# A hybrid attention block on one core: two key transposes come a projection chunk later, and two sets of branch weights are fetched tile by tile

## The chip, the core and the metric

The kernel runs on one core of a Trainium2 chip. TensorE (PE) multiplies matrices and transposes, VectorE (DVE), ScalarE (ACT) and GpSimd (POOL) work on rows of elements, and SyncE (SP) issues the transfers between the chip's memory and the core's own. Each engine goes through its own list of instructions in the order in which the program's scheduler put them, and waits there for semaphores of the others. The metric is the time of one execution in microseconds (us); lower is better.

## What is computed

One layer of a decoder block on 1024 tokens of width 1024, in float32. One projection of the normed input gives all that the two attention branches need; the branches are gated, merged and projected, and a SwiGLU feed-forward part follows.

```python
h = rmsnorm(x, norm_mix_g[l])
proj = h @ w_in[l]
(q_a, k_a, v_a, q_i, k_i, w_i, q_b, k_b, v_b, g) = split_columns(proj)
...
k_i = layernorm(k_i, idx_k_norm_g[l], idx_k_norm_b[l])
k_i = apply_partial_rope(k_i[:, :, None, :], cos_i, sin_i)[:, :, 0, :]
o_a = dsa_sparse_attention(q_a, k_a, v_a, q_i, k_i, w_i, n_top)
...
o_b = differential_attention(q_b, k_b, v_b, lam)
...
gates = jax.nn.sigmoid(g + gate_b[l]).reshape(B, S, N_BRANCH, D_MODEL)
merged = (gates[:, :, 0] * (o_a @ w_branch_dsa[l])
          + gates[:, :, 1] * (o_b @ w_branch_diff[l]))
x = x + merged @ w_out[l]
h = rmsnorm(x, norm_ffn_g[l])
gu = h @ w_ffn_in[l]
x = x + (jax.nn.silu(gu[..., :D_FF]) * gu[..., D_FF:]) @ w_ffn_out[l]
```

The sparse branch (DSA, 8 heads of 64) has an indexer: 8 small heads of width 32 score every earlier token (`relu(q_idx . k_idx)` weighted and summed), the 256 highest scores of each row are selected, and attention runs over those. The differential branch has 4 heads with two softmaxes each, whose difference weights the values.

## The kernel before

Every float32 product is made of three products of split operands: `x` is `hi + lo`, and the pairs (hi,hi), (hi,lo) and (lo,hi) of `PASS` are summed. To split a weight tile of 128x1024, ACT copies it to `whi` (L101), and POOL subtracts to get `wlo` (L102). `Weights.get` (L121 to L129) does the transfer (L125) and the split in one call.

**The projection stage.** There are 32 chunks for the queries and keys of both branches, 16 for the values and 16 for the gates. A query or key chunk is `chunk_mm` (L423 to L429): 24 products of 128x512 (L427) into one of the two accumulator banks `mm`, which an ACT copy (L468 for the first two chunks of a branch, L488 for the others) then reads out; DVE makes the low part of the later ones (L489). After each chunk `fill(5.2)` (L443) is called. Its first calls take a function out of the list `extra` (L441); later ones call `pump`, which feeds the indexer's work between the chunks: two pieces of `logits_gen` (the scores of one head) each time, and then as many pieces of `topk_gen` as fill the 5.2 us by its own table of costs. A piece of the top-k is a MAX8 (L299), which finds the eight highest values of each row, and a MATCH_REPLACE8 (L300), which takes them out, both on DVE; there are 176 such pairs. After the gates all that is left of them is run off, then attention starts.

Before the first scores, `idx_kT(0)` and `idx_kT(1)` (L227 to L237) must turn the indexer's keys: an ACT copy (`q`, L229), four PE transposes (L232), an ACT copy into `kst` (L235) and DVE subtractions. The keys come from `idx_keys`, a chain of DVE work (normalisation and rotation, its last instruction L188) that runs beside the first chunk.

**The attention stage.** There are 32 units for the differential branch (4 heads of 8 row blocks) and 64 for the sparse one. A unit's parts run with lags: scores and softmax at lag 0, transposes later, the product with the values at lag 4, and the closing part at lag 7. One loop over all units calls what is due. `diff_D` (L690 to L694) closes the last unit of a head: `finish_T` (L612) transposes the head's rows (L616) into `oT_hi` and `oT_lo` (L622, L623). At head 2 it also fetches the four tiles of `w_bdiff`, the differential branch's output weights. `dsa_D` (L756 to L776) closes the sparse units: at every third of them it makes half a column chunk of the differential branch's output (12 products, L767) out of these tiles, and at the end of `m` = 5 it fetches the four tiles of `w_bdsa`, which the sparse branch's output (`branch`, L625 to L631) needs right behind the last unit. The raw tiles stand in the pool `gst` under the name `gt`, which has two buffers; a head's rows (`rows_tile`, L641) and the gate tiles of the chunks (L761) take the same two.

Of the kernel before, what the change touches and what calls it, by code (L numbers as in the profile page):

```python
# [8 lines left out]
F32 = mybir.dt.float32  # L9
F32R = mybir.dt.float32r  # L10
# [8 lines left out]
P = 128  # L19
# [31 lines left out]
def block_kernel(ctx, tc, x, pos, g_mix, w_qk, w_v, q_scale, w_idx, w_gate, ikg, ikb, lams, sub_g, gate_b,  # L51
# [175 lines left out]
    def idx_kT(g):  # L227
        k4 = ip.tile([P, 4, 4, 32], F32, name="q4", bufs=1)
        A.activation(k4, IX[:, 4 * g:4 * g + 4, None, 256:288].to_broadcast([P, 4, 4, 32]), AF.Copy)  # L229
        tr = tr_bank()  # L230
        for j in range(4):
            T.transpose(tr[:, j, :], k4[:, j].rearrange("p a b -> p (a b)"), ident)  # L232
        ksl = kst[:, g * 512:(g + 1) * 512]
        tf = tr.rearrange("p a b -> p (a b)")
        A.activation(ksl, tf, AF.Copy)  # L235
        for q0 in (32, 96):
            V.tensor_sub(ksl[q0:q0 + 32], tf[q0:q0 + 32], ksl[q0:q0 + 32].bitcast(F32))  # L237
# [200 lines left out]

    fetch(0)
    fetch(1)  # L440
    extra = [lambda: idx_kT(0), lambda: idx_kT(1)]  # L441

    def fill(us):  # L443
        if extra:
# [245 lines left out]
    def diff_D(u):  # L690
        if u.last:
            finish_T(rows_of.pop((0, u.h)), u.h, sg[:, 0:1])
            if u.h == 2:
                u.wb.extend(W2.get(w_bdiff[k], raw=gst.tile([P, S], F32, name="gt")) for k in range(4))  # L694

    def dsa_A(u):
        sv, nh = scores(maps[1, u.m], u.t)
# [58 lines left out]
    def dsa_D(u):  # L756
        if u.chunk is not None:
            c, hf = u.chunk // 2, u.chunk % 2
            if hf == 0:
                u.fill.gt = gst.tile([P, S], F32, name="gt")  # L760
                nc.sync.dma_start(u.fill.gt, gate_dr[8 + c])  # L761
            gt = u.fill.gt[:, hf * 512:hf * 512 + 512]
            bt = mm_bank()
            n = 0
            for k in range(4):
                for a, b in PASS:
                    T.matmul(bt, lhsT=u.wb[k][b][:, c * P:(c + 1) * P],  # L767
                             rhs=oT[a][:, k, hf * 512:(hf + 1) * 512], start=n == 0, stop=n == 11)
                    n += 1
            V.tensor_mul(gt, bt, gt)  # L770
            nc.sync.dma_start(mb_dr[c][:, hf * 512:hf * 512 + 512], gt)
        if u.last and u.m == 2 * PARKED - 1:
            for h in range(PARKED):
                for dr, x_ in zip(o_dr, oT):
                    nc.sync.dma_start(x_[:, h, :].bitcast(F32), dr[h])
            wa.extend(W2.get(w_bdsa[k], raw=gst.tile([P, S], F32, name="gt")) for k in range(4))  # L776

    units, wbd, wa = [], [], []
    for h in range(4):
        for j, t in enumerate(ORDER):  # L780
            u = Unit()
            u.br, u.h, u.t, u.ext, u.first, u.last = 0, h, t, (t + 1) * P, j == 0, j == NT - 1
            u.wb = wbd
            u.f = ((1, diff_X), (0, diff_A0), (3, diff_B), (0, diff_A1), (4, diff_C), (7, diff_D))
            units.append(u)
    fill_ = Unit()
    for m in range(8):
        prs = {}
        for j, t in enumerate(ORDER2):
            u = Unit()  # L790
            u.pr = prs.setdefault(t // 2, Unit())
            u.pr.n = 0
            u.br, u.m, u.h, u.t, u.ext, u.first, u.last = 1, m, m // 2, t, (t + 1) * P, j == 0, j == NT - 1
            u.wb = wbd
            n = 8 * m + j
            u.fill = fill_
            u.chunk = n // EVERY if n % EVERY == 0 and n // EVERY < 2 * KC else None
            u.f = ((0, dsa_A), (1, dsa_X), (2, dsa_B), (4, dsa_C), (7, dsa_D))
            units.append(u)
# [576 lines left out]
```

## Time and profile before

| | |
|---|---|
| median of three runs | 1628.11 us (1628.06 to 1634.58) |
| the profiled execution, its own time | 1631.66 us |
| its span, first to last instruction | 1629.6 us |
| busy: PE, DVE, ACT, POOL | 95%, 71%, 41%, 35% |
| mean granted clock of PE | 0.99 |

The profile's times are those of one execution, counted from its first instruction; 2.06 us of its time lie outside the span. In a row of the timeline the start, the duration, the engine, the line and the operation are followed by what is written and read, and where the engine stood idle before it, by the length of that and what ended it.

### The profile page before, as it was taken

What the parts mean: (1) busy time and instruction counts of PE and PEld (TensorE: products, weight loads), DVE (VectorE), ACT (ScalarE), POOL (GpSimd) and SP (SyncE); (2) the same over time, 40 slices, a digit from 0 to 9 for tenths busy, and PEclk for the clock granted to TensorE, in tenths of its full rate; (3) what the DMA queues carried; (4) which work ended last, traced back from release to release, by engine and by line L of the source; (5) the groups of instructions that cost most, each with busy time, mean ns of one, the idle gap of its engine ahead of it and who ended that gap; (6) DMA issues with size and microseconds to landing.
All of it is one profiled execution on the core that took longest, in us unless ns stands there. A gap on an engine that the chain in (4) does not pass through costs nothing. (4 is left out here: it accounts for less than half of the span.)

```text
span 1629.6 us, 22639 instructions
## 1 busy us (share of the span) xinstructions
PE 1549.3 (95%) x8204; PEld 1319.4 (81%) x8204; DVE 1165.1 (71%) x1880; ACT 670.2 (41%) x1199; POOL 570.4 (35%) x465
## 2 busy tenths in 40 slices
PE   7799999999999998899999989999999999999997
PEld 6688779998888787788788977788787878887886
DVE  6479999989999998788772377555555555745553
ACT  5444541222211887777831243233232322443343
POOL 2442611342210024222421126666566666203311
PEclk9899999999999999999999999999999999999999
DMA  5243243348521466775384132444344445885532
GB/s 173 80 142 119 84 148 123 100 140 230 144 91 52 104 140 146 185 194 158 136 283 169 40 116 107 154 163 165 136 168 153 165 154 194 313 317 181 168 130 104
DMA packets 108079, 247.45 MB, mean 152 GB/s; under 512 B 12480, under 2 KB 30016, under 8 KB 107968
## 3 DMA queue, kind: packets, MB, share of 16 engines
q1 hardware_dynamic: 107968, 246.02, 46.2%
q8 instruction: 64, 1.05, 0.3%
q14 instruction: 47, 0.39, 0.1%
HBM read 167.06 MB, written 78.91 MB: 151 GB/s over the span
## 5 line engine op out<-in xcount | busy, mean ns | idle before, releaser
L102 POOL TENSOR_TENSOR alo<-r,ahi 128x512 fp32r<-128x512 f32 x152 | 206.4, 1366 | 165.3 <-ACT ahi L101 159.7
L102 POOL TENSOR_TENSOR wlo<-raw,whi 128x1024 fp32r<-128x1024 f32 (+1 forms) x49 | 117.5, 2404 | 310.0 <-ACT whi L101 300.6
L101 ACT ACTIVATE ahi<-r 128x512 fp32r<-128x512 f32 x152 | 95.5, 631 | 259.7 <-PE tr L1061 88.1
L1061 PE MATMUL tr<-blk,ahi 128*128 128x512 f32 x528 | 165.4, 394 | 9.2 <-DVE r L1073 8.5
L299 DVE MAX8 m<-score 128x8 f32<-128x640 f32 (+5 forms) x176 | 162.6, 924 | 5.4 <-POOL score L283 0.4
L300 DVE MATCH_REPLACE8 score<-m,score 128x640 f32<-128x640 f32 (+5 forms) x176 | 159.5, 906 | 0.0
L102 DVE TENSOR_TENSOR blk<-r,blk 128x1024 fp32r<-128x1024 f32 x77 | 101.6, 1352 | 73.8 <-ACT blk L101 73.6
L101 ACT ACTIVATE whi<-raw 128x1024 fp32r<-128x1024 f32 (+1 forms) x52 | 53.5, 1032 | 202.7 <-issue 97.7
L1061 PEld LDWEIGHTS tr<-blk,ahi 128*128 128x128 f32 x528 | 98.8, 189 | 33.6 <-DVE r L1073 11.9
L101 ACT ACTIVATE blk<-r 128x1024 fp32r<-128x1024 f32 x77 | 78.1, 1053 | 108.4 <-PE big L1277 44.4
L1061 PE MATMUL big<-blk,ahi 128*128 128x512 f32 x352 | 109.1, 391 | 0.9 <-DVE blk L102 0.9
L427 PE MATMUL mm<-hT_hi,whi 128*128 128x512 f32 x256 | 102.2, 399 | 5.6 <-DVE st_lo L489 5.6
L1061 PE MATMUL mm<-blk,ahi 128*128 128x512 f32 x336 | 104.3, 391 | 0.4 <-ACT r L1070 0.3
L1061 PE MATMUL tr<-blk,alo 128*128 128x512 f32 x264 | 103.6, 393 | 0.6 <-POOL alo L102 0.6
L427 PE MATMUL mm<-hT_lo,whi 128*128 128x512 f32 x256 | 100.6, 393 | 0.0
L427 PE MATMUL mm<-hT_hi,wlo 128*128 128x512 f32 x256 | 100.3, 392 | 0.0
L427 PE MATMUL big<-hT_hi,whi 128*128 128x512 f32 x256 | 99.6, 389 | 0.0
L427 PE MATMUL big<-hT_lo,whi 128*128 128x512 f32 x256 | 99.6, 389 | 0.0
L427 PE MATMUL big<-hT_hi,wlo 128*128 128x512 f32 x256 | 99.6, 389 | 0.0
L1277 PE MATMUL big<-blk 128*128 128x512 f32 x396 | 91.8, 391 | 1.8 <-DVE r L1245 1.5
L1277 PEld LDWEIGHTS big<-blk 128*128 128x128 f32 x396 | 73.8, 188 | 19.5 <-issue 1.9
L592 PE MATMUL big<-khs,qs 128*128 128x512 f32 (+4 forms) x192 | 74.4, 389 | 5.3 <-DVE mx L701 2.5
(286 smaller groups left out, 3973.9 us busy)
## 6 DMA issues: line engine op xcount, KB each, us to landing
r<-in_w_ffi_dram SPq DMA_DIRECT2D x44, 512.0 KB, 4.5
r<-in_w_ffo_dram SPq DMA_DIRECT2D x22, 512.0 KB, 4.8
tdr<-r SPq DMA_DIRECT2D x22, 512.0 KB, 2.6
sdr<-r SPq DMA_DIRECT2D x44, 256.0 KB, 2.6
r<-sdr SPq DMA_DIRECT2D x44, 256.0 KB, 4.0
r<-tdr SPq DMA_DIRECT2D x44, 256.0 KB, 4.0
r<-actdr SPq DMA_DIRECT2D x33, 256.0 KB, 4.1
r<-in_w_ffo_dram SPq DMA_DIRECT2D x33, 256.0 KB, 5.2
```

The source lines that it names most:

```text
L101: A.activation(hi, src, AF.Copy)
L102: lo_eng.tensor_sub(lo, src, hi.bitcast(F32))
L299: tc.keep_in_program_order(V.max(m8, work[t]))
L300: V.match_replace(work[t], m8, work[t], GONE)
L427: T.matmul(dst, lhsT=w[b][:, k * P:(k + 1) * P], rhs=hT[a][:, k, u * 512:(u + 1) * 512], start=n == 0, stop=n == 23)
L592: T.matmul(sp_[:, u, :n], lhsT=q[:, t * P:(t + 1) * P], rhs=kh_[:, cols], start=True, stop=False)
L1061: T.matmul(banks[z], lhsT=w[b][:, k * P:(k + 1) * P], rhs=o[:, a, k, :], start=first and m == 0, stop=last and m == 11, skip_group_check=True)
L1277: T.matmul(bs_[r], lhsT=v[:, a, r * P:(r + 1) * P], rhs=v[:, b, 512:], start=p in OPEN and j == 0 and m == 0, stop=p in SHUT and j == NP - ...
```

## The change

The list of the first fills gets an empty entry in front: the first fill does nothing, the key transposes come with the second and third, and all of the pumping starts one chunk later. And the two fetches of four weight tiles are taken apart by a new function `step`: `n` counts the units from the head's last one on, an even `n` from 0 to 7 issues one tile's transfer, and the odd one behind it does that tile's split, so that four tiles spread over eight units. The number of instructions and bytes is the same.

```diff
-    extra = [lambda: idx_kT(0), lambda: idx_kT(1)]
+    extra = [lambda: None, lambda: idx_kT(0), lambda: idx_kT(1)]
...
     def diff_D(u):
         if u.last:
             finish_T(rows_of.pop((0, u.h)), u.h, sg[:, 0:1])
-            if u.h == 2:
-                u.wb.extend(W2.get(w_bdiff[k], raw=gst.tile([P, S], F32, name="gt")) for k in range(4))
+        step(u.wb, w_bdiff, 8 * u.h + u.j - 23)
+
+
+    def step(wb, src, n):
+        if 0 <= n < 8 and n % 2 == 0:
+            wraw[0] = gst.tile([P, S], F32, name="gt")
+            nc.sync.dma_start(wraw[0], src[n // 2])
+        elif 0 <= n < 8:
+            hi = W2.pool.tile([P, 1024], F32R, name="whi", bufs=W2.n)
+            lo = W2.pool.tile([P, 1024], F32R, name="wlo", bufs=W2.n)
+            tc.keep_in_program_order(A.activation(hi, wraw[0], AF.Copy))
+            G.tensor_sub(lo, wraw[0], hi.bitcast(F32))
+            wb.append((hi, lo))
+
+    wraw = [None]
...
-            wa.extend(W2.get(w_bdsa[k], raw=gst.tile([P, S], F32, name="gt")) for k in range(4))
+        step(wa, w_bdsa, 8 * u.m + u.j - 8 * PARKED * 2 + 1)
```

The scheduler orders each engine's list anew, so the place of the rows is read from the built programs.

ScalarE behind the projection's first two weight tiles: `L229` are the copies ahead of the key transposes, `L409` is a small constant with its table load, `L468` reads a chunk's bank out.

```order
-L229 ACTIVATE q_723<-ix 128x512
+L229 ACTIVATE q_750<-ix 128x512
 L409 ACT_TABLE_LOAD
 L409 ACTIVATE lsm<-lsm 128x2
+L468 ACTIVATE xx<-mm,qs 128x512 x2
+L235 ACTIVATE kst<-tr 128x512
+L229 ACTIVATE q_801<-ix 128x512
+L101 ACTIVATE st_hi<-ra 128x512
+L101 ACTIVATE st_hi<-xx 128x512
+L101 ACTIVATE whi<-raw 128x1024
 L468 ACTIVATE xx<-mm,qs 128x512
 L235 ACTIVATE kst<-tr 128x512
```

The copy for the keys stands at the same place; behind it both of the first chunks are now read out before `kst`, where it was one. On TensorE it is likewise: the second chunk's 24 products stand ahead of the first transposes L232, not behind them.

The transfers that SyncE issues around the four tiles of `w_bdiff` (`qs`, `khs`, `kls` and `vt` are the next heads' queries, keys and values, `odr` parked results). Before:

```order
-L125 DMA gt<-in_w_bdiff_dram 128x1024
-L538 DMA khs<-qkh_77 64x1024
-L539 DMA kls<-qkl_79 64x1024
-L537 DMA qs<-qkl_79 64x1024
-L125 DMA gt<-in_w_bdiff_dram 128x1024
-L538 DMA khs<-qkh_77 64x1024
-L539 DMA kls<-qkl_79 64x1024
-L537 DMA qs<-qkh_77 64x1024
-L125 DMA gt<-in_w_bdiff_dram 128x1024
-L538 DMA khs<-qkh_77 64x1024
-L539 DMA kls<-qkl_79 64x1024
-L546 DMA vt<-vsdr 128x8x128
```

and now, where the second, third and fourth tile are issued:

```order
+L538 DMA khs<-qkh_77 64x1024
+L539 DMA kls<-qkl_79 64x1024
+L546 DMA vt<-vsdr 128x8x128
+L699 DMA gt<-in_w_bdiff_dram 128x1024 x2
+L767 DMA odr_82<-so_6273 64x256
+L767 DMA odr_83<-so_6274 64x256
+L767 DMA odr_82<-so_6358 64x256
+L767 DMA odr_83<-so_6359 64x256
+L537 DMA qs<-qkh_77 64x1024
+L699 DMA gt<-in_w_bdiff_dram 128x1024
```

The second to fourth tile came between the loads of the sparse branch's first head and held them up; now these loads and `vt` go first, and the second and third tile are issued together behind them, the fourth after four small stores.

TensorE at the first chunk of the differential branch's output (`L767`, in the changed kernel `L780`; `L616` is `finish_T` of the last head; `L726` and now `L739` are transposes of the sparse units, `L739` and now `L752` their products with the values). Before, from `finish_T` to the last product of the chunk:

```order
L616 MATMUL tr<-ident,gt 128x128 x8
L767 MATMUL mm<-oT_hi,wlo 128x512
L593 MATMUL big<-kls,qs 128x448
L592 MATMUL big<-khs,qs 128x384
L593 MATMUL big<-kls,qs 128x384
L726 MATMUL tr<-ident,pm 128x128 x5
L767 MATMUL mm<-oT_hi,whi 128x512
L767 MATMUL mm<-oT_lo,whi 128x512
L739 MATMUL mm<-wide,vt 128x256
L592 MATMUL big<-khs,qs 128x512
L593 MATMUL big<-kls,qs 128x512
L767 MATMUL mm<-oT_hi,wlo 128x512
```

and now, where the products of its second tile and the ones behind it stand:

```order
L592 MATMUL big<-khs,qs 128x384
L739 MATMUL tr<-ident,pm 128x128 x2
L780 MATMUL mm<-oT_hi,whi 128x512
L780 MATMUL mm<-oT_lo,whi 128x512
L739 MATMUL tr<-ident,pm 128x128 x4
L780 MATMUL mm<-oT_hi,wlo 128x512
L739 MATMUL tr<-ident,pm 128x128 x2
L780 MATMUL mm<-oT_hi,whi 128x512
L780 MATMUL mm<-oT_lo,whi 128x512
L780 MATMUL mm<-oT_hi,whi 128x512
L780 MATMUL mm<-oT_lo,whi 128x512
L780 MATMUL mm<-oT_hi,wlo 128x512
```

Before, eight of the chunk's twelve products stood ahead of `finish_T` and four behind it, the second chunk's twelve some way on in one piece. Now two stand ahead of `finish_T` and ten behind it, mixed with those of the second chunk, and both chunks end at the same place. From `branch` on TensorE's list is the same as before.

## Rows read from the trace of the kernel before

**Rows 1.** The page's busy times: us, share of the span, instructions.

```profile
PE 1549.3 (95%) x8204; PEld 1319.4 (81%) x8204; DVE 1165.1 (71%) x1880; ACT 670.2 (41%) x1199; POOL 570.4 (35%) x465
```

**Rows 2.** Windows: busy us (instructions) of PE, PEld, DVE, ACT, POOL; then clock, DMA.

```profile
66.00:68.00 2.00, 2.00 (x6) 1.57 (x5) 1.27 (x2) 1.20 (x3) 1.65 (x2) 0.50 0.00 0
120.00:520.00 400.00, 394.36 (x2119) 342.36 (x2119) 383.85 (x563) 113.59 (x151) 109.62 (x66) 1.00 0.39 125
...
650.00:662.00 12.00, 7.52 (x31) 4.88 (x30) 7.41 (x17) 9.22 (x19) 7.40 (x9) 0.87 0.65 170
662.00:665.00 3.00, 3.00 (x15) 2.84 (x14) 1.95 (x7) 1.81 (x6) 0.00 (x0) 0.50 0.30 121
780.00:815.00 35.00, 31.61 (x193) 26.02 (x192) 26.33 (x69) 29.56 (x70) 18.08 (x24) 0.95 0.37 134
815.00:1620.00 805.00, 783.67 (x3820) 656.00 (x3819) 449.24 (x518) 265.59 (x395) 334.86 (x239) 1.00 0.48 169
```

**Rows 3.** Timeline of PE from the first chunk's end to the third chunk's start.

```profile
55.65 0.39 PE L427 MATMUL mm<-hT_lo,whi 128*128 128x512 f32 x1
55.88 0.39 PE L427 MATMUL mm<-hT_hi,wlo 128*128 128x512 f32 x1
64.15 1.12 PE L232 MATMUL tr<-ident,q 128*128 128x128 f32 x4 [7.89 <-ACT q L229]
...
65.49 0.63 PE L427 MATMUL mm<-hT_lo,whi 128*128 128x512 f32 x1
65.92 0.63 PE L427 MATMUL mm<-hT_hi,wlo 128*128 128x512 f32 x1
...
72.51 0.47 PE L427 MATMUL mm<-hT_hi,whi 128*128 128x512 f32 x1
```

**Rows 4.** Timeline of DVE, ACT and POOL beside it.

```profile
62.98 0.45 DVE L188 TENSOR_TENSOR ix<-rope_a,rope_b 128x288 f32<-128x288 f32 x1
...
63.47 0.63 ACT L229 ACTIVATE q<-ix 128x512 f32<-128x512 f32 x1 [6.69 <-DVE ix L188]
...
65.52 0.67 ACT L468 ACTIVATE xx<-mm,qs 128x512 f32<-128x512 f32 x1
...
47.31 4.76 POOL L102 TENSOR_TENSOR wlo<-raw,whi 128x1024 fp32r<-128x1024 f32 x2 [9.49 <-ACT whi L101]
```

**Rows 5.** Timeline of DVE: one wait late in the projections, and the top-k's end.

```profile
362.21 0.94 DVE L300 MATCH_REPLACE8 score<-m,score 128x768 f32<-128x768 f32 x1
367.48 0.84 DVE L528 CAST causw<-caus 128x128 bf16<-128x128 f32 x1 [4.32 <-DMA vsdr<-st_lo]
...
531.03 0.69 DVE L305 TENSOR_SCALAR bias<-score 128x1024 bf16<-128x1024 f32 x1
532.62 1.23 DVE L650 CUSTOM_DVE_ANT_0 pm<-big,causw 128x1024 f32<-128x1024 f32 x1 [0.90 <-PE big L593]
```

**Rows 6.** Timeline of PE where the gates end and attention starts.

```profile
531.18 0.40 PE L427 MATMUL big<-hT_hi,wlo 128*128 128x512 f32 x1
```

**Rows 7.** Timeline of SP, ACT and POOL: the last two tiles of `w_bdiff`.

```profile
653.66 0.33 SPq L125 DMA_DIRECT2D gt<-in_w_bdiff_dram  x1
...
650.12 1.06 ACT L101 ACTIVATE whi<-gt 128x1024 fp32r<-128x1024 f32 x1 [3.23 <-DMA gt<-in_w_bdiff_dram]
...
658.00 1.06 ACT L101 ACTIVATE whi<-gt 128x1024 fp32r<-128x1024 f32 x1 [1.31 <-DMA gt<-in_w_bdiff_dram]
...
659.13 2.38 POOL L102 TENSOR_TENSOR wlo<-gt,whi 128x1024 fp32r<-128x1024 f32 x1 [2.04 <-ACT whi L101]
```

**Rows 8.** Timeline of PE: the first two chunks of the differential branch's output.

```profile
661.57 0.79 PE L767 MATMUL mm<-oT_hi,wlo 128*128 128x512 f32 x1 [0.17 <-POOL wlo L102]
...
669.74 0.39 PE L767 MATMUL mm<-oT_hi,wlo 128*128 128x512 f32 x1
```

**Rows 9.** Timeline of SP and ACT: the last three tiles of `w_bdsa`.

```profile
784.20 12.89 SPq L125 DMA_DIRECT2D gt<-in_w_bdsa_dram  x3
...
800.28 1.06 ACT L101 ACTIVATE whi<-gt 128x1024 fp32r<-128x1024 f32 x1 [1.37 <-DMA gt<-in_w_bdsa_dram]
```

More of the change, by code (lines that the diff above doesn't have):

```diff
@@ L782, in block_kernel @@
             u.br, u.h, u.t, u.ext, u.first, u.last = 0, h, t, (t + 1) * P, j == 0, j == NT - 1
+            u.j = j
             u.wb = wbd
@@ L793, in block_kernel @@
             u.br, u.m, u.h, u.t, u.ext, u.first, u.last = 1, m, m // 2, t, (t + 1) * P, j == 0, j == NT - 1
+            u.j = j
             u.wb = wbd
```

## The prediction

> **What bounds the kernel now.** The page's busy times come first: TensorE is busy for 1549.3 of 1629.6 us [rows 1], so what can be won is some 80 us of its idle time and the time in which it ran at half clock. The windows then tell where. Behind 815 us TensorE is busy for 783.67 of 805 us [rows 2], and its list there is unchanged: that stretch can be shifted, not shortened. From 120 to 520 us, where the projections, the indexer's scores and the top-k lie, TensorE is busy for 394.36 of 400 us and DVE for 383.85 [rows 2]: two engines are full at once, and neither alone sets the time. The two tie at the end too: the last product of the gates ends at 531.58 (531.18 and 0.40, [rows 6]), the last step of the top-k at 531.72 (531.03 and 0.69), and the first softmax of attention starts at 532.62 after 0.90 us in which DVE waits for scores [rows 5]. The three places of the change are at 50 to 75, 627 to 670 and 770 to 815 us.
>
> **The transposes.** The timeline of TensorE shows a stall at 56.27: the first chunk's last product ends there (55.88 and 0.39), and the transposes L232 start at 64.15 after 7.89 us of waiting for the ACT copy `q` [rows 3]. The copy itself waited 6.69 us for the last step of the keys on DVE, which ends at 63.43 [rows 4]. Nothing in the change makes that step earlier. But the second chunk no longer stands behind the transposes: its weights were split by 52.07 (47.31 and 4.76, [rows 4]) and its bank is the free one of two. Its 24 products, 0.23 us apart (55.65 to 55.88, [rows 3]), take 5.5 us, so they run from 56.3 to 61.8, and the stall is 2.35 us instead of 7.89. The transposes then start at 64.15 as before. The third chunk uses the first tile again, but needs the first chunk's bank, which ACT has read out at 66.19 (65.52 and 0.67, [rows 4]): it starts at 66.2, where it was 72.51 [rows 3]. TensorE gains **6.3 us** there.
>
> The clock is the first thing that could take from it. After the stall the granted clock was 0.50, the lower of the two levels (1.2 GHz), between 66 and 68 us [rows 2], and products took 0.63 instead of 0.39 us, 0.43 apart [rows 3]; some ten of them were slow, which is 10 x 0.20 = 2.0 us. The new stall is a third as long, with a second of about one microsecond behind it. I leave the 2.0 us where they are: with no fall at all it would be 2 more, the gain 8.3.
>
> How much of this reaches attention is decided by DVE, since the top-k must be done first. The change takes nothing off DVE; what it can win is its waits, and work that comes earlier. The top-k starts when the first scores are there. These come one chunk later in the list (5.5 us) on a TensorE that is 6.3 us earlier: some 1 us of gain at the start. Next, DVE stands 4.32 us at L528, waiting for the transfers that end the value chunks [rows 5]; these move with TensorE. In the changed program's DVE list 109 MAX8 stand ahead of L528, where it was 111, so DVE arrives two pairs earlier (some 2 us each, the MATCH_REPLACE8 half took 0.94, [rows 5]) and has them still to do behind it. The wait becomes 0.7 to 1 us shorter at best. So the top-k ends about 2 us earlier, and TensorE's gates 6 us earlier. The scores are then ready before DVE is, so its wait of 0.90 us goes as well. Attention starts 2.9 us earlier, and TensorE stands idle there for some 3 us: there are few score banks that it can fill ahead. **Term 1: −2.9 us**; the bounds are 0, if DVE was as full as it can be, and −6.3, if DVE turns out to wait for TensorE in more places than I count.
>
> **The tiles of `w_bdiff`.** In the kernel before, the four tiles go one after the other through one buffer, each waiting for POOL's split of the one before. The last is issued at 653.66, its ACT copy starts at 658.00 after 1.31 us of waiting, and POOL splits it from 659.13 to 661.51 [rows 7]: one round of issue, landing, copy and split is 7.9 us. TensorE waits for this split: the last product of the first chunk starts at 661.57 [rows 8], and the second chunk is done at 670.13 [rows 8]. From 650 to 662 TensorE is busy for only 7.52 of 12 us, and the clock falls: it is 0.50 from 662 to 665, in which 15 instructions fill 3.00 us [rows 2]. So this place costs some 4.5 us of idle time and 1.5 of slow work. ACT, too, is held: it stood 3.23 us at the third tile's copy [rows 7], with `finish_T`'s copies and the softmax's exponentials behind it in its list.
>
> In the new order SyncE first issues the loads of the sparse head and `vt`, then tiles two and three together, and ACT's copies of tiles two to four come behind `finish_T`'s. So `finish_T` no longer waits behind a copy that waits for a transfer: I put it at 650 instead of 653. The third tile lands some 4.3 us behind that (653.66 to 658.00, [rows 7]), at 654.4; POOL ends the second tile's split at 658 and the third's at 660.3. The fourth tile needs the second's buffer, is issued at 658, and by the same round its split ends at 666 (658 and 7.9). The first chunk's last product is thus 4.4 us later than before, but the second chunk's twelve are no longer a block behind it: they are done tile by tile beside the first's, and one or two products are left when the last split comes. Both chunks are done at about 667 instead of 670.1. **Term 2: −3.0 us**, bounds −4.5 (all the idle time) and +2 (a split that comes 5 us later than I put it).
>
> **The tiles of `w_bdsa`.** The last three are issued together from 784.20 on, held for 12.89 us until `gst` buffers come free; the last copy waits 1.37 us, at 800.28 [rows 9]. `branch` starts right behind. From 780 to 815 TensorE is idle for 3.4 of 35 us, and the clock's mean is 0.95 [rows 2]. In the new order three are still issued together, but in ACT's list of the changed program the copies stand 16 to 19 places later and let exponentials go first. **Term 3: −1.0 us**, bounds 0 and −3.
>
> Against this stand no added instructions. The sum is −6.9 us: 1624.8 for the profiled execution of 1631.66. That one lies 3.55 above the median, and I carry the difference over to it: 1628.11 − 6.9 = 1621.2, which I give as 1621.
>
> **The rivals.**
>
> *The top-k hides all of the first gain.* DVE is busy for 96% of the 400 us; if the waits that remain are not TensorE's, term 1 is 0 and the time 1624. Against it speaks the 0.90 us that DVE did wait for scores.
>
> *The whole gain of TensorE survives.* If DVE is late because its inputs were, the 6.3 us carry to attention: 6.3 + 3 + 1 gives 1617.8. For it speaks that DVE waits at L528 for transfers that move with TensorE; against it that the top-k's 176 pairs are not fewer.
>
> *The split tiles come too late, slower.* The third tile's transfer waits for `finish_T`, the fourth's for the second's split, and both splits stand in line on POOL. If each ACT copy is held by another 3.23 us, as one was before [rows 7], the last split ends at 666 + 6.5 = 672.5. TensorE has the products of tiles two to four in list order, so it stands behind the first that is late, and both accumulator banks are held. Then the second chunk ends at 673.5, 3.4 later than before, and if the products left run 0.20 us slow, as above, it is 5 to 6 with some ten to twelve of them. With terms 1 and 3 this is 1628.11 + 5.5 − 3.9 = 1629.7. It turns into a loss for this place when the last split ends behind 669.6, and for the kernel when that is behind 673.
>
> *The clock falls at the new waits.* Idle time moves to the start of attention (3 us) and in between the chunks' tiles. If each of these lets the clock fall for as long as the stall at 56 us did, 2.0 us at one place and 1 to 2 at the other go back: 1621 + 3.5 = 1624.5. The trace bears it out so far in that both stalls of before were followed by a granted clock of 0.50 [rows 2]. The Trainium skill, "TensorE: Matmul & The Clock Gate", section "HAM oscillation — how this bites in real kernels", says that bursts of products with waits for data in between start cold each time, and would so speak against a chunk cut into four pieces; the trace agrees with it at both places, and has no row for pieces as short as these.
>
> **How the numbers follow.** The forecast has a chance of 0.38 (1618.5 to 1623.5 around 1621), the top-k's cover 0.13 (1624), TensorE's whole gain 0.24 (1617.8, and below with the bounds of terms 2 and 3), the late tiles 0.15 (1629.7), the clock 0.10 (1624.5). 0.5% is 8.1 us, about what a measurement of this kernel tells from no change: faster is below 1620.0. That holds for most of TensorE's whole gain and for four tenths of the forecast: 0.24 x 0.95 + 0.38 x 0.4, with a little from elsewhere 0.39. Slower by as much, above 1636.2, would take late tiles at twice the price: 0.03. The rest is 0.58. The range runs from 1614 (6.3, 4.5 and 3 together, 1614.3) to 1629, which leaves out half of the late tiles and a little at the lower end.
>
> **What would show it.** In the profile after: the stall ahead of L232 near 2.4 us and the third chunk at 66; the first softmax some 3 us earlier, TensorE waiting for DVE there; the last split of `w_bdiff` near 663 and both chunks done by 664, once the 2.9 us are taken off; `branch` 6 to 7 us earlier. The prediction is wrong if attention starts at the old place or 6 earlier, or if TensorE waits at L780 for a split for over 3 us.

## The result and the profile after

The changed kernel takes 1618.96 us in the median of 4 runs (1614.87 to 1619.83), beside 1629.18 us before in the same comparison: a ratio of 0.9926 with a 95% interval of 0.9897 to 0.9954, or 10.2 us by the medians and 12.1 by the ratio (its interval is 7.5 to 16.8). The profiled execution has a span of 1617.9 us, 11.7 below that of before.

Read in the order of the prediction. TensorE is busy for the same time in a shorter span (page of the changed kernel; compare [rows 1]):

```profile
PE 1548.1 (96%) x8204; PEld 1318.3 (81%) x8204; DVE 1156.8 (71%) x1880; ACT 669.1 (41%) x1199; POOL 568.7 (35%) x465
```

Its timeline from the second chunk's end to the third chunk's start (compare [rows 3]):

```profile
61.84 0.39 PE L427 MATMUL mm<-hT_hi,wlo 128*128 128x512 f32 x1
64.87 1.11 PE L232 MATMUL tr<-ident,q 128*128 128x128 f32 x4 [2.65 <-ACT q L229]
66.96 0.79 PE L427 MATMUL mm<-hT_hi,whi 128*128 128x512 f32 x1 [0.98 <-ACT xx L468]
67.56 0.63 PE L427 MATMUL mm<-hT_lo,whi 128*128 128x512 f32 x1
```

The stall ahead of L232 is 2.65 us where it was 7.89, with 0.98 more ahead of the third chunk. That chunk starts at 66.96. In this execution the keys were done 0.72 us later than before (their last step ends at 64.15, before at 63.43), so against the keys it came 6.3 us earlier: 72.51 − 63.43 = 9.08 before, 66.96 − 64.15 = 2.81 now. Of these, 0.35 us are a change of order: before, the second four transposes stood ahead of the third chunk, and now they stand behind it (they start at 74.44). Products of 0.63 us follow at a granted clock of 0.50 (68 to 70 us), so the clock fell as before.

DVE's timeline where the projections end, at two of the bias copies L305, and at the top-k's end (compare [rows 5]), and TensorE's last product of the gates (compare [rows 6]):

```profile
360.69 0.83 DVE L528 CAST causw<-caus 128x128 bf16<-128x128 f32 x1 [4.42 <-DMA vsdr<-st_lo]
...
366.97 0.56 DVE L305 TENSOR_SCALAR bias<-score 128x768 bf16<-128x768 f32 x1
...
441.62 0.63 DVE L305 TENSOR_SCALAR bias<-score 128x896 bf16<-128x896 f32 x1
...
524.88 0.69 DVE L305 TENSOR_SCALAR bias<-score 128x1024 bf16<-128x1024 f32 x1
525.91 1.23 DVE L650 CUSTOM_DVE_ANT_0 pm<-big,causw 128x1024 f32<-128x1024 f32 x1 [0.34 <-PE big L593]
...
524.47 0.40 PE L427 MATMUL big<-hT_hi,wlo 128*128 128x512 f32 x1
```

The wait at L528 is as long as before (4.42, 4.32 before) but ends 6.8 us earlier. The first softmax starts at 525.91, 6.7 us earlier, and DVE waits only 0.34 us ahead of it; the gates end at 524.87, before the top-k (525.57). The two L305 in the middle take 0.56 and 0.63 us. What they took before was not among the rows ahead of the prediction; here they are, with POOL beside them, in the timeline of the kernel before:

```profile
369.67 2.47 DVE L305 TENSOR_SCALAR bias<-score 128x768 bf16<-128x768 f32 x1
...
446.22 2.19 DVE L305 TENSOR_SCALAR bias<-score 128x896 bf16<-128x896 f32 x1
...
369.32 2.40 POOL L102 TENSOR_TENSOR wlo<-raw,whi 128x1024 fp32r<-128x1024 f32 x1 [1.08 <-ACT whi L101]
...
445.52 2.40 POOL L102 TENSOR_TENSOR wlo<-raw,whi 128x1024 fp32r<-128x1024 f32 x1 [8.46 <-ACT whi L101]
```

Each begins while POOL is at a split of a weight tile, takes 2.47 and 2.19 us, and ends 0.4 to 0.5 us behind the split.

The windows of the changed kernel, TensorE's columns first, then the clock behind POOL's columns (compare [rows 2]; the later ones are moved by the 6.7 us):

```profile
120.00:520.00 400.00, 397.67 (x2130) 345.70 (x2129) 383.27 (x566) 113.98 (x153) 107.65 (x66) 1.00 0.40 125
...
643.00:655.00 12.00, 9.39 (x54) 7.01 (x54) 10.33 (x24) 10.60 (x23) 7.48 (x11) 1.00 0.39 118
655.00:664.00 9.00, 7.37 (x42) 5.96 (x43) 4.31 (x12) 4.62 (x10) 3.42 (x4) 1.00 0.50 151
773.00:808.00 35.00, 31.39 (x191) 25.11 (x190) 24.89 (x65) 27.41 (x66) 17.56 (x24) 1.00 0.41 146
```

From 120 to 520 us TensorE is idle for 2.3 us where it was 5.6. That difference is not one of the two kernels: in the run e2_steps, whose list is that of before up to attention, the same window has 2.4 us of idle time.

```profile
120.00:520.00 400.00, 397.61 (x2131) 345.77 (x2130) 382.28 (x566) 114.50 (x154) 110.16 (x66) 1.00 0.39 125
```

At the differential branch's first two chunks it is busy for 9.39 of 12 us instead of 7.52, and the clock stays at 1.00.

The same place in the timelines of SP, ACT, POOL and PE (compare [rows 7, 8]):

```profile
635.33 9.54 SPq L699 DMA_DIRECT2D gt<-in_w_bdiff_dram  x2
...
652.60 0.33 SPq L699 DMA_DIRECT2D gt<-in_w_bdiff_dram  x1
...
649.04 1.07 ACT L703 ACTIVATE whi<-gt 128x1024 fp32r<-128x1024 f32 x1
...
651.02 1.04 ACT L703 ACTIVATE whi<-gt 128x1024 fp32r<-128x1024 f32 x1
...
658.36 1.06 ACT L703 ACTIVATE whi<-gt 128x1024 fp32r<-128x1024 f32 x1
...
650.20 5.11 POOL L704 TENSOR_TENSOR wlo<-gt,whi 128x1024 fp32r<-128x1024 f32 x2
...
659.50 2.38 POOL L704 TENSOR_TENSOR wlo<-gt,whi 128x1024 fp32r<-128x1024 f32 x1 [3.49 <-ACT whi L703]
...
643.27 1.10 PE L616 MATMUL tr<-ident,gt 128*128 128x128 f32 x8 [1.00 <-POOL gt L688]
...
652.63 0.50 PE L780 MATMUL mm<-oT_hi,wlo 128*128 128x512 f32 x1 [1.22 <-POOL wlo L704]
...
655.36 0.49 PE L780 MATMUL mm<-oT_hi,wlo 128*128 128x512 f32 x1 [0.62 <-POOL wlo L704]
...
661.93 0.73 PE L780 MATMUL mm<-oT_hi,wlo 128*128 128x512 f32 x2 [1.27 <-POOL wlo L704]
```

The second and third tile are issued together from 635.33 on, the issue of the third ending 9.54 us later; POOL splits both from 650.20 to 655.31, and the fourth, issued at 652.60, until 661.88. TensorE waits three times for a split, 1.22, 0.62 and 1.27 us, and both chunks end at 662.66, where it was 670.13.

### The profile page after: what moved, and what is told of

Same layout as the page of the kernel before. It is cut to its first block, busy times and chain, and to the rows that moved or that the text cites. A ratio compares the mean times of both kernels' runs of the same rounds, so it can differ in the third digit from the quotient of the medians.

```text
span 1617.9 us, 22643 instructions
## 1 busy us (share of the span) xinstructions
PE 1548.1 (96%) x8204; PEld 1318.3 (81%) x8204; DVE 1156.8 (71%) x1880; ACT 669.1 (41%) x1199; POOL 568.7 (35%) x465
## 5 line engine op out<-in xcount | busy, mean ns | idle before, releaser
L1076 PEld LDWEIGHTS big<-blk,ahi 128*128 128x128 f32 x352 | 66.0, 188 | 15.8 <-DVE blk L102 1.7
```

The lines of the kernel that those rows point to most:

```text
L1076: T.matmul(banks[z], lhsT=w[b][:, k * P:(k + 1) * P], rhs=o[:, a, k, :], start=first and m == 0, stop=last and m == 11, skip_group_check=True)
```

## The experiments

Times are medians of several runs, and the ratio is to runs of the kernel before on the same chip. For comparison between executions I count from the moment at which the keys are done (the end of L188 on DVE), because that moment itself lies between 63.4 and 66.2 us from one execution to the next. This table is worked out from the rows of each run's trace as they are shown for two of them above: the start of the first MAX8, the end of the wait at L528, the ends of the top-k and of the gates, and the start of the first softmax.

| kernel | first MAX8 | L528 | top-k ends | gates end | first softmax |
|---|---|---|---|---|---|
| before | 41.68 | 304.05 | 468.29 | 468.15 | 469.19 |
| e2_steps | 41.04 | 301.72 | 465.19 | 465.05 | 466.10 |
| e3_diff | 41.47 | 305.44 | 469.49 | 469.33 | 470.38 |
| e4_dsa | 41.11 | 301.26 | 465.29 | 465.14 | 466.19 |
| e8_before_pool | 42.17 | 302.70 | 461.47 | 466.55 | 467.70 |
| changed | 39.01 | 296.54 | 461.42 | 460.72 | 461.76 |
| e1_keys | 39.52 | 297.33 | 462.21 | 461.27 | 462.45 |
| e7_collide | 38.69 | 296.53 | 461.64 | 460.46 | 461.88 |
| e9_two_inputs | 39.06 | 296.72 | 462.33 | 460.80 | 462.57 |
| e5_nostall | 46.49 | 294.60 | 469.64 | 458.63 | 469.88 |
| e6_nostall_pool | 46.44 | 295.12 | 464.17 | 458.55 | 467.92 |
| e10_lead | 38.16 | 297.79 | 461.97 | 461.83 | 462.88 |
| e11_after_lead | 31.48 | 298.71 | 454.60 | 462.85 | 463.90 |

The second table counts from the first softmax: the start of the last `finish_T`, the end of the sixteenth differential chunk, and the end of `branch`.

| kernel | `finish_T` | 16 chunks | `branch` ends |
|---|---|---|---|
| before, e1_keys, e8_before_pool | 119.8 to 120.4 | 247.0 to 247.6 | 319.8 to 320.5 |
| e4_dsa | 120.0 | 246.4 | 318.0 |
| e3_diff | 117.2 | 245.1 | 318.1 |
| changed, e2_steps | 117.2 to 117.4 | 245.1 to 245.3 | 317.0 to 317.2 |

**The parts alone.** In the first run only the line of `extra` is changed:

```diff
-    extra = [lambda: idx_kT(0), lambda: idx_kT(1)]
+    extra = [lambda: None, lambda: idx_kT(0), lambda: idx_kT(1)]
```

> Only the key transposes come a chunk later; both weight fetches are as before. Theory A (the whole gain of TensorE reached attention, because DVE's own work in front of it also became shorter: two copies L305 no longer ran beside a POOL instruction): the first softmax starts near 526 us, 6 to 7 earlier, the two L305 take about 0.6 us each, and the time falls by 6 to 8 us. Theory B (the trace of the change showed one lucky execution; in general the top-k hides most, as the prediction had it): the first softmax starts near 529.5, the time falls by 3 us.

Measured: 1621.92 us, ratio 0.9959 (0.9942 to 0.9976), 6.7 us. The first softmax is where the changed kernel has it, and both L305 are short again. The other three leave that line as it was and take `step` in both places, in `diff_D` alone, or in `dsa_D` alone.

```diff
-            if u.h == 2:
-                u.wb.extend(W2.get(w_bdiff[k], raw=gst.tile([P, S], F32, name="gt")) for k in range(4))
+        step(u.wb, w_bdiff, 8 * u.h + u.j - 23)
...
-            wa.extend(W2.get(w_bdsa[k], raw=gst.tile([P, S], F32, name="gt")) for k in range(4))
+        step(wa, w_bdsa, 8 * u.m + u.j - 8 * PARKED * 2 + 1)
```

> Only the two weight fetches are taken apart; the key transposes are as before. Theory A: the rest of the measured gain, 3 us: finish_T of the last head 3 us earlier, the last differential chunk 2.3 us earlier, branch 3 us earlier. Theory B: 4 us, what the prediction summed for both places. A rival: the parts need each other (the fetches gain only when attention starts earlier), then this run is within 1 us of before.

> Only the four tiles of w_bdiff are fetched step by step. Theory A, from the ends of the sixteen differential chunks in the trace of the change: -2.3 us at the last chunk, so 2 to 3 us in all. The rival of the late tiles: slower by 1.5 us.

> Only the four tiles of w_bdsa are fetched step by step. Theory A: 0.7 us faster at the first product of branch, 0 to 1 in all. A rival, that the 1.5 us by which the end of the change's trace moved more than branch did come from here: 2 us or more.

Measured: both 0.9976 (0.9964 to 0.9989), 3.9 us; `w_bdiff` alone 0.999 (0.9978 to 1.0003), 1.6 us; `w_bdsa` alone 0.9986 (0.9968 to 1.0004), 2.3 us. The two single ones are not clear of zero by the clock of the runs. Their traces show more: `finish_T` comes 3 us earlier where `w_bdiff` is stepped, and nowhere else; `branch` ends 2 us earlier with either, 3.2 with both. For `w_bdsa` alone that is more than the 0.7 expected of it. 6.7 and 3.9 are 10.6, beside 10.2 by the medians and 12.1 by the ratio: within intervals as wide as these (3.9 to 9.4 and 1.8 to 5.9) the parts add, and the late tiles are no loss.

**TensorE without the stall at the transposes.** A second empty entry, and ACT's copies kept in the order in which they are written, so that the banks are read out before the keys are awaited:

```diff
+    extra = [lambda: None, lambda: None, lambda: idx_kT(0), lambda: idx_kT(1)]
...
+                tc.keep_in_program_order(A.activation(xx[c], pt, AF.Copy, scale=qs[:, 0:1]))
...
+        tc.keep_in_program_order(A.activation(k4, IX[:, 4 * g:4 * g + 4, None, 256:288].to_broadcast([P, 4, 4, 32]), AF.Copy))
```

> The changed kernel, with a second empty entry ahead of the key transposes and with ScalarE's reading of the first banks kept ahead of the keys' copy, so that TensorE does not stand at the transposes at all. Theory A (in the changed kernel the top-k on DVE is level with TensorE, so that TensorE alone can win no more): the stall of 2.65 us and the half clock behind it are gone, TensorE's gates end 4 to 6 us earlier against the keys, but the first softmax moves by less than 1.5 us and the time by less than 2 us against the changed kernel, which is 9 to 12 below before. The rival (attention starts when TensorE is done): 4 to 6 us below the changed kernel, 14 to 17 below before.

Measured: 1628.5 us, ratio 0.9987 (0.9968 to 1.0006). The first softmax is 8.1 us later than in the changed kernel, and neither theory had that. Timeline of PE and DVE, the third chunk's start, the gates' last product, two copies L305 and the first softmax:

```profile
65.08 0.50 PE L427 MATMUL mm<-hT_hi,whi 128*128 128x512 f32 x1 [3.00 <-ACT xx L468]
...
522.25 0.40 PE L427 MATMUL big<-hT_hi,wlo 128*128 128x512 f32 x1
...
371.31 2.76 DVE L305 TENSOR_SCALAR bias<-score 128x768 bf16<-128x768 f32 x1
...
448.16 2.20 DVE L305 TENSOR_SCALAR bias<-score 128x896 bf16<-128x896 f32 x1
...
533.90 1.22 DVE L650 CUSTOM_DVE_ANT_0 pm<-big,causw 128x1024 f32<-128x1024 f32 x1 [0.23 <-DVE bias L305]
```

The stall ahead of the transposes is gone, but one of 3.00 us stands ahead of the third chunk: ACT reads the banks out only behind L409, which waited 6.02 us for DVE. The clock stayed at 1.00 there (60 to 80 us). Against the keys the gates end 2.1 us earlier than in the changed kernel, not 4 to 6. Attention waits 11 us more for the top-k. The first MAX8 came 7.5 us later (46.49 against 39.01), so that at L528, which is even 1.9 us earlier, three pairs more are left to do (106 MAX8 stand ahead of it, 109 in the changed kernel); and two L305 take 2.76 and 2.20 us, 3.8 more than in the changed kernel. The rival is out: attention does not start when TensorE is done. The next run moves the bias copies to POOL:

```diff
-                V.tensor_scalar(bias[t], work[t], GONE, BIG, op0=OP.not_equal, op1=OP.mult)
+                G.tensor_scalar(bias[t], work[t], GONE, BIG, op0=OP.is_gt, op1=OP.mult)
+                G.affine_select(bias[t][:, t * P:], bias[t][:, t * P:], pattern=[[-1, P]], compare_op=OP.is_ge,
+                                fill=BIG, base=0, channel_multiplier=1)
```

> The same, with the making of the bias (L305, one pass over the scores of each of six row blocks) moved from DVE to POOL with a small instruction behind it for later tokens. Theory A: DVE loses 3 us of its own work at least, and the first softmax comes 2 to 3 us earlier than in the run before, 12 to 15 below before in all. The rival (L305 costs nothing, other work fills its place): as the run before within 1 us.

Measured: 1626.92 us, 0.998 (0.9965 to 0.9994). DVE ended its top-k 5.5 us earlier, but the softmax only 2.0, since it then waited 3.75 us for the last of these copies, on POOL.

The same move in the kernel before:

> The kernel before, with the bias made on POOL as above: the long copies L305 are gone, and DVE with them is 5 us less busy. Theory A (before, TensorE's gates end level with the top-k, so that DVE alone can win no more): the first softmax comes 1 us earlier at most, the time is within 1.5 us of before. The rival (before, the top-k alone set the start of attention): 4 to 5 us faster.

Measured: 1627.33 us, 0.9981 (0.9967 to 0.9995), 3.1 us. The top-k ended 461.5 us behind the keys, as early as in the changed kernel, but TensorE's gates at 466.6, and the first softmax waited 6.22 us for its scores:

```profile
531.23 1.23 DVE L652 CUSTOM_DVE_ANT_0 pm<-big,causw 128x1024 f32<-128x1024 f32 x1 [6.22 <-PE big L595]
```

So before, TensorE was in the way as well: the top-k's 6.8 us gave 1.5 at this point, no more than the gates' 1.6. The time's 3.1 us are more than that; their interval reaches down to 0.8.

**Useless POOL work beside L305.** In the changed kernel, two POOL instructions on scores that are used up:

```diff
+                if t in (5, 6):
+                    for _ in range(2):
+                        G.tensor_sub(work[4], work[4], m8[:, 0:1].to_broadcast([P, 640]))
                 V.tensor_scalar(bias[t], work[t], GONE, BIG, op0=OP.not_equal, op1=OP.mult)
```

> The changed kernel, with two useless POOL subtractions of 128x640 (on scores that are used up) put beside the copies L305 of the row blocks 5 and 6: they start with the block's last MAX8 and last some 3 us. Theory A (a copy L305 cannot run while POOL is at work, and this is what the kernel before paid): each of the two L305 takes 2 us or more instead of 0.6, ends behind POOL, the top-k ends 3 to 4 us later, and the time is 3 to 4 us above the changed kernel, 6 to 8 below before. The rival (the long L305 had another cause): both stay at 0.6 us and the time is that of the changed kernel, 10 below before.

Measured: 1618.79 us, 0.9937 (0.9915 to 0.9959), the time of the changed kernel. In the timeline of DVE and POOL the copy is here L308. POOL's two instructions are one row of 2.78 us; the last row is the first of them alone:

```profile
366.98 0.66 DVE L308 TENSOR_SCALAR bias<-score 128x768 bf16<-128x768 f32 x1
...
365.97 2.78 POOL L307 TENSOR_TENSOR score<-score,m 128x640 f32<-128x640 f32 x2 [1.21 <-DVE m L299]
...
365.97 1.25 POOL L307 TENSOR_TENSOR score<-score,m 128x640 f32<-128x640 f32 x1 [1.21 <-DVE m L299]
```

Theory A's size failed. But the copy is not a free one: it starts 0.24 us before POOL's first instruction ends, at 367.23, takes 0.66 us instead of 0.56, and ends 0.42 us behind it, as the copy of before ended behind the split (372.13 and 371.72). The second POOL instruction did not hold it. So this run could cost no more than 0.1 us, and it does not decide whether POOL work with a tile and one column holds a copy as work with two whole tiles does. The next run was put as a test of that difference:

```diff
+                if t in (5, 6):
+                    G.tensor_sub(work[4][:, :8], work[4][:, :8], m8)
+                    for _ in range(2):
+                        G.tensor_sub(work[4], work[4], work[4])
```

> The changed kernel, again with useless POOL work beside the copies L305 of the row blocks 5 and 6, this time with instructions that read two whole tiles, as the splits of weights do: a small one of 8 columns behind the block's last MAX8, then two subtractions of 128x640. Theory A, narrowed (a DVE copy of this kind does not start while POOL is at an instruction that reads two whole tiles; the earlier POOL work read one tile and a column): each of the two L305 ends behind POOL and takes 2 us or more, the top-k ends 3 to 4 us later against the keys, the first softmax 2.5 to 3.5 later, and the time lies 2 to 4 us above the changed kernel. The rival (the long copies had another cause): 0.6 us each, the time of the changed kernel.

Measured: 1621.55 us, 0.9945 (0.9925 to 0.9965). Timeline of DVE (the copy is L309) and POOL:

```profile
367.27 0.94 DVE L309 TENSOR_SCALAR bias<-score 128x768 bf16<-128x768 f32 x1
...
366.54 2.79 POOL L308 TENSOR_TENSOR score<-score 128x640 f32<-128x640 f32 x2
...
366.54 1.25 POOL L308 TENSOR_TENSOR score<-score 128x640 f32<-128x640 f32 x1
```

The copy takes 0.94 us instead of 0.56; the other one 0.88 instead of 0.63. POOL's first instruction ends at 367.80 (the last row), and the copy, begun at 367.27, ends 0.42 behind that: it got in between the two. It is held to the end of the POOL instruction that is running, not of all that follow, and so the cost was 0.8 us at the first softmax, not 3. The run differs from the one before in when the copy meets POOL's first instruction, 0.53 us before its end here and 0.24 there; in both it ends 0.42 us behind. So the pair of runs shows the hold, but not that the number of whole tiles decides.

**A head start for the top-k.** The first three pumping calls give four heads' scores each:

```diff
-            pump(us, 2)
+            lead[0] -= 1
+            pump(us, 4 if lead[0] >= 0 else 2)
+
+    lead = [3]
```

In the kernel with two empty entries, and in the changed kernel as it is:

> The kernel without TensorE's stall and with one chunk more ahead of the keys (two empty entries), and the first three pumping calls feed four heads' scores each in place of two, so that the top-k starts two to three chunks earlier. Theory A (attention starts when both the top-k and TensorE's gates are done; in the run with two empty entries the top-k was 11 us behind TensorE): the first MAX8 comes 10 us or more earlier than in that run, the first softmax follows TensorE's gates within 1.5 us, 459 to 461 us behind the keys where it was 469.9, and the time is 1 to 3 us below the changed kernel. The rival (the top-k's end does not follow its start, because DVE waits elsewhere): within 2 us of that run.

> The changed kernel as it is, with the same three fuller pumping calls. Theory A (in the changed kernel the two engines end level, so an earlier top-k alone wins little): the first MAX8 4 us or more earlier, the first softmax 0.5 to 1.5 us earlier, the time within 1.5 us of the changed kernel. The rival (the top-k alone sets the start): 4 us or more faster.

Measured: 1621.33 us, 0.9939 (0.9917 to 0.996), and 1622.56 us, 0.9947 (0.993 to 0.9964). The first MAX8 came 8.3 and 7.5 us earlier than without it. In the first, top-k and gates ended level again, at 461.97 and 461.83, in spite of two L305 of 2.41 and 2.2 us that were back; but the gates were 3.2 us later than without the head start. In the second the top-k was done 8 us before the gates, and the first softmax stood 9.30 us waiting for TensorE, whose gates had become 2.1 us later. In both the times that were expected, up to 3 us below the changed kernel and within 1.5 us of it, were missed: neither beats the changed kernel.

## Why the prediction was right, and which term was too small

The forecast was 1621 and a gain of 6.9; measured were 1618.96 and 10.2, inside the range. The direction and the three places were right; term 1 was mis-sized. That the time is inside owes something to the width of the range, which reached down to 1614 for the case that TensorE's whole gain survives.

**The stall and TensorE's 6.3 us** were right to the decimal: 6.27 against the keys, the stall 2.65 for 2.35, the second wait 0.98 for about one, and the half clock stayed, with nine slow products where the trace of before has eight (the prediction counted some ten). The 6.27 contain the 0.35 us of the second transposes, which the prediction did not count.

**Term 1, −2.9, measured −6.7** (e1_keys, 3.9 to 9.4 by its interval). The step that failed is "the change takes nothing off DVE", from which it followed that "the wait becomes 0.7 to 1 us shorter at best. So the top-k ends about 2 us earlier". The start of the top-k was put 1 us earlier and came 2.0 earlier. The two pairs fewer ahead of L528 were there (109 of them, 111 before). But the wait at L528 did not shrink. Both its sides moved: the transfers came 6.8 us earlier with TensorE, and DVE was there 6.9 us earlier, 2.0 by its start and the rest by the two pairs (3.9 us) and by its score sums L277, which took 3.0 us less, 41.1 instead of 44.1 for 35 of them; some 2 us went to other work and waits. DVE's own earlier arrival decides nothing there, since it then waits 4.42 us. Behind L528, where the two pairs had to be made up, the way to the end grew by only 0.64 us (164.24 and 164.88), since the three L305 took 1.9 us instead of 5.4. In the groups of DVE by line, up to the wait and behind it, of the kernel before:

```profile
L277 DVE SCALAR_TENSOR_TENSOR score<-rl,ix,score 128x512 f32<-128x512 f32 (+4 forms) x35 | 44.1, 1259 | 1.3
...
L305 DVE TENSOR_SCALAR bias<-score 128x768 bf16<-128x768 f32 (+2 forms) x3 | 5.4, 1784 | 0.1
```

and of the changed kernel:

```profile
L277 DVE SCALAR_TENSOR_TENSOR score<-rl,ix,score 128x512 f32<-128x512 f32 (+4 forms) x35 | 41.1, 1175 | 1.6
...
L305 DVE TENSOR_SCALAR bias<-score 128x768 bf16<-128x768 f32 (+2 forms) x3 | 1.9, 627 | 0.1
```

Without these 3.5 us, by this count, the top-k of the changed kernel would have ended at 529.1, 2.7 us earlier than before: about what the prediction said. What it missed is that DVE's own work behind L528 became shorter.

The rest is less sure. Executions of the list of before are of two kinds, and the trace of before is of one of them. Against it the change brings the first softmax 7.4 us forward, counted from the keys; against e2_steps and e4_dsa, whose list up to attention is the same, only 4.3 to 4.4, and L528 4.7 to 5.2 instead of 7.5. In these two the seven sums L277 of 1024 columns take 9.0 us, as in the changed kernel, where they take 12.5 before and in e3_diff. So of the 3.0 us of L277 most is not shown to come from the change. For the copies L305 it is shown: the one of 896 columns takes 2.18 or 2.19 us in all four traces of the old list, and 0.63 in the changed kernel.

**Why it became shorter.** A copy L305 or score sum of DVE that starts while POOL is at an instruction with two inputs (a split is one) ends behind that instruction. In the thirteen traces 178 such copies and sums start so, and all of them end behind it, by a time that is set by their size: 0.41 or 0.42 us for the copies of 768 columns, 0.48 to 0.52 for those of 896, 1.08 or 1.09 for the sums of 1024. Those that start at another time take 0.56, 0.63 and 1.27 to 1.29 us. A sum L277 beside a split, in the timeline of DVE and POOL of the kernel before:

```profile
229.50 3.24 DVE L277 SCALAR_TENSOR_TENSOR score<-rl,ix,score 128x1024 f32<-128x1024 f32 x1
...
229.20 2.46 POOL L102 TENSOR_TENSOR wlo<-raw,whi 128x1024 fp32r<-128x1024 f32 x1 [10.28 <-ACT whi L101]
```

In all four traces with the old list up to attention (before, e2 to e4) L305 of block 5 takes 1.7 to 2.5 us beside a split; in the changed kernel and e1_keys, where no POOL instruction of two inputs is running, it takes 0.56. The hold was shown by making it come back in part (e9_two_inputs). A POOL instruction that reads one tile does not hold a sum: in e8_before_pool, where POOL makes the bias, a sum L277 of 1024 columns lies inside that work and takes its usual 1.28 us, and so does one in e6_nostall_pool.

```profile
234.87 1.28 DVE L277 SCALAR_TENSOR_TENSOR score<-rl,ix,score 128x1024 f32<-128x1024 f32 x1
...
234.38 1.93 POOL L305 TENSOR_SCALAR bias<-score 128x512 bf16<-128x512 f32 x1 [14.87 <-DVE score L300]
```

That the new list keeps L305 clear of the splits is no aim of the change: two more pairs stand ahead of it behind L528, and the split is over by then. It is luck of the order: with the lists of e5_nostall and e10_lead, which also bring the transposes later, both copies are long again (2.76 and 2.20, 2.41 and 2.20 us).

The Trainium skill, "Advanced Engine Details and Errata", section "VectorE Performance Modes", has a note that the second port of DVE is shared with GpSimd, so that GpSimd's instructions and those of DVE in a two-port mode block each other. The traces agree for L305; L277 is held in the same way, and no row here shows in which mode it runs. For MAX8 and MATCH_REPLACE8 they show no lengthening: in the timeline of the changed kernel a MAX8 that lies wholly beside a split takes 1.09 us, the mean of its size, and the MATCH_REPLACE8 that begins beside the same split takes 1.08, also its mean.

```profile
439.30 1.09 DVE L299 MAX8 m<-score 128x8 f32<-128x896 f32 x1
...
438.81 2.41 POOL L102 TENSOR_TENSOR wlo<-raw,whi 128x1024 fp32r<-128x1024 f32 x1 [8.47 <-ACT whi L101]
```

The prediction never looked for it. The durations of L305 alone, 0.69 us for 1024 columns [rows 5] and 2.47 for 768, would have shown that there were some 3.5 us to lose or win.

**The rivals.** TensorE's whole gain survived by the runs, at 6.7 of 6.3 with an interval of 3.9 to 9.4: the case that had 0.24. It did not survive for the reason given there alone. e8_before_pool shows that a top-k 6.8 us earlier gives 1.5 us when the gates gain only 1.6, and in e5_nostall TensorE's gates were 9.5 us earlier than before and attention no earlier, since the top-k was late. In every row of the table the first softmax comes 0.2 to 1.2 us behind the later of gates and top-k, but for e6_nostall_pool, where POOL's copy is later than both. The change moved both, by 7.4 and 6.9 us against the trace of before.

**Term 2, −3.0, measured −2.1** at the third chunk (it ends 142.8 us behind the first softmax, before 144.9) and 2.3 at the sixteenth, in e3_diff much as in the changed kernel. Against e4_dsa, which fetches these tiles as before, it is 1.0 and 1.1. `finish_T` 3 us earlier was right to 0.1 us. The fourth split was put too early: counted from the first softmax the forecast had it end at 133.4 (666 − 532.6), and it ended at 136.0 (661.88 − 525.91), so both chunks were done at 136.8 instead of 134.4, and 137.5 before. Only 0.8 us was won there, and against e4_dsa (136.5) nothing; the rest shows at the third chunk, and what brought it there no run here takes apart. **Term 3, −1.0, measured −1.0** with `w_bdiff` stepped as well (`branch` ends at 318.1 with that alone, at 317.1 with both), and −1.8 to −2.5 alone. The late tiles did not come as a loss: the last split was 2.6 us late, where 3.6 (669.6 less 666) would have turned this place, and TensorE's three waits for POOL are 3.1 us together.

**The clock rival** did not come, and at the tiles the clock moved the other way. Between 643 and 664 us the granted clock is 1.00 although the chunks are cut in pieces with waits between, where it was 0.50 from 662 to 665 in the kernel before [rows 2]. At the start of attention it is 1.00 too (524 to 529 us). The waits of 0.62 to 1.27 us did not bring the clock down. The section of the Trainium skill cited there tells of longer waits than these, so that it is not contradicted: the prediction took it to pieces for which it had no row.

In the profiled execution the end moved by 1.7 us more than `branch` did. From the end of `branch` to TensorE's last product the traces of all these kernels differ by 5 us (761.9 to 767.0), the lowest in e8_before_pool and e4_dsa and the highest in the kernel before and e10_lead, so nothing of the change is read from it.

## What to carry to other kernels

Where two engines end a stage level, look for the instruction at which one waits for the other late in it: a gain of the releasing engine passes there in full, as long as the waiting one arrives early enough, and what is left behind that point, in count and in duration, decides the rest. Compare the durations of one instruction at several sizes in the row of each form: a shorter one that takes three times as long is held by something, here by POOL's instructions of two inputs, and a change of order can take the hold away or bring it. When a test is to bring a hold back, check in the trace how much of the holding instruction was left when the held one started. Moving one engine's work forward by delaying another's pays only until the two are level; one chunk further lost 8 us here, 3.8 of them in copies that were held again. And take the trace of before more than once: here two of four traces of one list differ from the other two by 3 us.

## What was not expected of the hardware

A DVE copy of 768 columns took 0.56 us alone and up to 2.76 us (e5_nostall) when it began during a POOL subtraction. It ends 0.41 or 0.42 us behind that subtraction wherever it began, and it slips in between two POOL instructions in a row. MAX8 and MATCH_REPLACE8 are not held.

A stall of TensorE of 3.00 us left the granted clock at 1.00 (e5_nostall); two of 2.65 and 0.98 us with four transposes between them were followed by 0.50 (the changed kernel).

Executions of one list differ by more than the change's smaller terms: the keys are done between 63.4 and 66.2 us, and from there to the first softmax the list of before took 469.2, 470.4, 466.1 and 466.2 us. The 3 us between lie where TensorE is busy for 74.36 or for 77.61 of the 80 us from 180 to 260, and the score sums L277 of 1024 columns take 12.5 or 9.0 us for the seven of them in the same traces. It is the same hold by POOL: in two of the traces (before and e3_diff) two of the seven sums start 0.3 to 0.7 us behind the start of a split and end 1.08 us behind its end; in the other two the longest of the seven takes 1.38. What decides between the two kinds is open, and so is whether the new list avoids the held sums or had them by chance in none of its four traces (changed, e1, e7, e9). Measured against the kind without them the key transposes gave 4.3 us, against the kind with them 7.4.
